# Turning differential attention's stacks and summing its head norms with float32r products

## The chip, the cores and the metric

One core of a Trainium2 chip runs the whole program in one launch. The metric is device time in microseconds (us) of that core. Three runs of the kernel before gave 1991.06, 1992.38 and 1996.98 us; their median is 1992.38 us.

Five engines matter here. TensorE (PE) multiplies: a stationary tile is loaded into the array (the profile calls this load PEld) and a moving tile is streamed past it. VectorE (DVE) and ScalarE (ACT) do element-wise work, and each engine works through its own instructions in their order in the program. SyncE (SP) issues the transfers.

## The reference

Two layers act on 256 latent tokens and 256 context tokens of width 1024, in float32. Each layer is a half-step SwiGLU, a mixer and a second half-step SwiGLU, each behind an RMS norm that is shifted and scaled. The mixer runs four groups of heads side by side on one input projection and joins them in one output projection. The change touches two of the groups. In short:

```
# differential attention: 8 score heads of 32 features make 4 output heads of 64
q, k = rope(rms(q)), rope(rms(k))
o    = softmax(q0 k0) v - lam * softmax(q1 k1) v      # for each pair of score heads
y    = rms(o) * subln * (1 - lam_init)                # a "head norm"
# HGRN2: a gated two-way scan of 4 heads of 64 value features
y    = rms(o) * out_norm * silu(g)                    # the other "head norm"
# both of them, with latent attention and grouped attention
x    = x + gate * concat(y...) @ mix_w_out
```

In the last layer the mixer gives only the latent half, 256 tokens instead of 512.

## The kernel before

**Dense products.** Activations and weights are kept as two float32r parts, hi and lo, and a dense product is three float32r products (`mm3`, or its like in `tokmajor`): hi by hi, hi by lo, lo by hi. Feature tiles are 128 rows by up to 512 tokens. `split` (line 246) makes the two parts: ACT copies a tile to float32r, and DVE subtracts that copy from the source.

**The mixer** (line 1026) is a long stream of dense products (`dense()`: the input projection, `mixin` in the trace, then the output projection, `mixo`) with chains of dependent steps woven into it. A chain is a generator that stops between its steps. Class `Weave` (line 101) writes the order: it keeps one clock for each of PE, DVE and ACT, adds a rough price for each instruction (`Engine.price`, line 70: 0.11 for a transpose, 0.00042 per column of a product, four times that where its moving operand is float32), adds a price per hop from one engine to another, and runs a chain's next step once its results should be there by those clocks. At most 4 chains (layer 0) or 3 (layer 1) are open at a time. A scheduler then places the instructions of every engine. So a changed instruction changes the clocks, and with them the order of everything woven in.

**The chains of this change.** In `da` (line 1148), `stack` writes for each tile of 128 tokens and each of two groups of four score heads a tile that holds q or k of a head as hi and lo parts, 4 times 32 columns; the parts are exact float32r numbers. `to_feat` (line 951) turns the k stacks and line 1187 the q stacks: a `transpose` on PE against the fp32 identity (`cst` in the trace), 128x128 each, four to a PSUM tile. In the trace these are `da0~pb<-cst,da0~g` and `da1~pb<-cst,da1~g`, one for each layer. `unit` (line 966) then makes the scores (`dau~ps`), the softmax, the transposes of the probabilities (`dau~pb<-cst,dau~g`) and the products with the values. When all units of a pair of output heads are done, `headnorm` (line 893) is spawned: ACT squares the pair's tile, PE multiplies the squares by a block matrix of ones (`self.blk`, also in `cst`) in one fp32 product, ACT makes `rstd` of the sums by a logarithm and an exponential, DVE scales. There are four head norms in a layer, `y0` and `y1` (differential attention, also called by its tile `da0~g` in the trace) and `y4` and `y5` (HGRN2, `hg0` and `hg1` in the trace).

**The output projection** takes its eight k tiles in two parts: 2, 3, 0, 1, 4, 6 and then 7, 5 (`MO` and `PARTS`). Tiles 2 and 3 come from latent attention, 6 and 7 from grouped attention (`gqa0`, `gqau`). Each part has eight output tiles. A first-part tile accumulates 18 products; four PSUM banks are open for them, so 4 times 15 products can run before tile 6 is there. In layer 0 a product has 512 columns, in layer 1 it has 256.

Of the kernel before, what the change touches and what calls it, by code (L numbers as in the profile page):

```python
# [15 lines left out]
P = 128  # L16
D = 1024
KT = 8
# [5 lines left out]
# per layer: chains at a time, their margin behind the products, lead of the other engines, price of a hop  # L24
# [22 lines left out]
# columns of the broadcast row of small weights  # L47
# [11 lines left out]
# of the output projection: the k tiles of each part, and the feature tiles that share a piece of its weights  # L59
# [4 lines left out]
class Engine:  # L64
    """An engine of the core; adds up a rough cost of what it is given, to order independent chains."""
# [35 lines left out]
class Weave:  # L101
    """Interleaves a long stream of dense products with chains of dependent steps."""
# [14 lines left out]
    def step(self, gen, ready):  # L117
        """Run one step; the time at which its results are there, None at its end."""
# [51 lines left out]
class Net:  # L170
    def __init__(self, tc, I, O, ctx):
# [29 lines left out]
        self.blk = self.cst[:, C_BLK:C_BLK + P]  # L201
        self.eps = self.cp.tile([P, 1], F32, tag="eps", name="eps")
# [43 lines left out]
    def split(self, hi, lo, src):  # L246
        """hi + lo == src, both exact in float32r."""
        nc = self.nc
        nc.scalar.activation(hi, src, AF.Copy)
        nc.vector.tensor_sub(lo, src, hi.bitcast(F32))  # L250

    def weights(self, src, fine=1):
        """A [P, <= 1024] piece of a weight as its two exact float32r parts."""
# [11 lines left out]
    def table(self, name):  # L265
        """Load an activation table behind all that ScalarE has been given."""
        self.tc.keep_in_program_order(self.bass.scalar.preload_act_table_set(name))

    def copy(self, out, src, scale=None):
        """out = src * scale (a value per partition), on the engine that is behind."""  # L270
# [18 lines left out]
    def rstd(self, out, ssum, n):  # L289
        """out = (ssum / n + eps) ** -0.5"""  # L290
        nc = self.nc
        p = ssum.shape[0]
        nc.scalar.activation(out, ssum, AF.Ln, bias=self.eps[:p], scale=1.0 / n)
        nc.scalar.activation(out, out, AF.Exp, scale=-0.5)

# [1 line left out]
    def ada_fin(self, l, m, mod, rv, f):  # L297
        """Bias, norm weight and step on the features f of the products rv [P, f, s]."""
# [5 lines left out]
        if m % 3 == 1:  # L304
            # norm_w * (1 + scale)
# [15 lines left out]
    def turned(self, row):  # L321
        """[P, f * P] sums, four rows of them in use -> [P, f, P], features on the partitions."""
# [6 lines left out]
    def ada_first(self, q):  # L329
        """A list of closures; run in order they give quarter q of the features of mods[0, 1] and mods[0, 0];  # L330
        products on the tensor engine, a column group to each module and parity of the k tile."""
# [29 lines left out]
    def ada_units(self, l, m):  # L361
        """A list of closures; run in order they give mods[l, m] = [P, KT, 2] (products on VectorE)."""
# [42 lines left out]
    def stat(self, dt, cc, late=0):  # L405
        """Adds the squares of the columns cc of feature tile dt to the sums of the next norm."""
# [17 lines left out]
    def norm_rs(self, s):  # L424
        """1 / rms of the tokens of stream s, on all partitions."""
# [8 lines left out]
    def norm_apply(self, xh, xl, l, i, s, rs, ks):  # L434
        """Feature tiles ks of rms(x) * norm_w * (1 + scale) + shift of stream s in two float32r parts."""
# [10 lines left out]
    def norm_begin(self, l, i, c0):  # L446
        """The next normed and modulated streams: the latents now, the context at norm_end."""
# [18 lines left out]
    def residual(self, ps, gate, dt, s, stat, late=0):  # L466
        """X += gate * ps on stream s."""
# [7 lines left out]
    def parts(self, c0, halves):  # L475
        """Column ranges to run one after the other and their streams."""
# [7 lines left out]
    def ffn(self, l, j, c0, filler, final=False):  # L484
# [12 lines left out]
        def fill(t):  # L497
            """Runs what is due of the filler after another t of the time it is spread over."""
# [11 lines left out]
        def up(fts, order, ws=None):  # L510
            """Hidden tiles fts side by side; order: the steps (k tile, columns). Yields after each step."""
            pss = [(self.psa(), self.psa()) if n < 2 else (self.psb(), self.pss()) for n in range(len(fts))]
            ws = ws or {}
            # a start marks the whole bank as unwritten: one is enough where the halves take turns
# [19 lines left out]
        def open_up():  # L534
            """The first tiles while the shift and scale of the second half of the features come in."""
# [87 lines left out]
    def mix_setup(self, l):  # L623
        """Small weights of layer l on every partition, rotary tables with the norm weights in them."""
# [8 lines left out]
        # T1, T2: [P, tt, qk, d]  # L633
# [15 lines left out]
        # lambda  # L649
# [12 lines left out]
        # subln * (1 - lam_init), hg_out_norm per partition (64-feature rows twice)  # L662
# [6 lines left out]
    def lb_setup(self):  # L669
        """Lower bounds of the last layer: softmax over the two layers, [P, dir, head]."""  # L670
# [22 lines left out]
    def feats(self, srcs, cs, halves=False):  # L693
        """Pairs of feature-major [128, N] tiles of the combined input projection, from columns cs on."""
# [23 lines left out]
    def tokmajor(self, src, ncol, c_ctx, then, banks=None):  # L718
        """Token-major columns, ctx tokens from column c_ctx on; src(i) the i-th pair of k tiles.
        then(tt, ps) gets each token tile."""  # L720
# [18 lines left out]
    def sigmoid(self, e, f, x):  # L739
        """f = 1 / (1 + exp(-x)) with the functions of one table, e = exp(-x) (both within 1e-19 of 0)."""  # L740
# [11 lines left out]
    def hgrn_gate(self, l, h, i, ps, c0):  # L752
        """q (i = 0) or the gates f and keys k of direction i - 1, [dk, tokens]."""
# [15 lines left out]
    def hgrn_head(self, l, h, q, F, K, o, last):  # L769
        """The scan of a head as attention whose decays are products of gates over halving blocks."""  # L770
# [15 lines left out]
        def blocks(ps, A, B):  # L786
            """The products of the keys A and queries B of each block of 32: ps[key, tile, query of the block]."""
# [10 lines left out]
        for li, b in enumerate(LEVELS):  # L798
# [11 lines left out]
            else:  # L810
                # the keys of 64 with the queries of the second and of the first part of them (b = 32), or of the
                # other 64: together the whole tiles, but for the blocks of 32 on the diagonal
# [11 lines left out]
            # to blocks of 2 b  # L824
# [25 lines left out]
        # now blocks of 128: between the two tiles of a stream  # L850
# [7 lines left out]
        # from the context to the latents  # L858
# [14 lines left out]
        # values  # L873
# [19 lines left out]
    def headnorm(self, key, o, w, c0, gates=None, n=0):  # L893
        """RMSNorm of each of a pair of 64-feature heads on the partitions."""
        nc = self.nc
        self.ph = key
        sq, rs = self.g([P, N]), self.g([P, N])
        nc.scalar.activation(sq[:, c0:], o[:, c0:], AF.Square)
        yield
        self.ph = key  # L900
        ps = self.psb()
        nc.tensor.matmul(ps[:, c0:], self.blk, sq[:, c0:], start=True, stop=True)
# [9 lines left out]
    def rot(self, out, zn, t1, t2, nh, d):  # L912
        """out = rotary(zn * w); out, zn: [P, nh, d]; tables [P, d]."""
# [10 lines left out]
    def heads_norm(self, src, nh, d):  # L924
        """src (PSUM) [P, nh * d] -> src / rms over d, [P, nh, d]."""
# [10 lines left out]
    def qk_tok(self, n, tt, ps, o, nq, nk, d, out):  # L936
        """Norm, weight and rotate the q and k heads of a token tile; out: [P, nq + nk, d]."""
# [12 lines left out]

    def to_feat(self, dst, toks, cols, np_, mask=None):
        """dst [np_, N] = transpose of toks[tt][:, cols]; toks[tt] may be None. With a mask, dst[i] keeps
        the rows that column i of it names."""
# [3 lines left out]
        for t in range(t0, 4):  # L957
            nc.tensor.transpose(ps[:np_, t], toks[t][:, cols], self.ident)
# [525 lines left out]
```

## Time and profile before

| what | value |
|---|---|
| runs | 1991.06, 1992.38, 1996.98 us, median 1992.38 us |
| span of the profiled execution, first to last instruction | 1989.2 us |
| PE busy | 1943.7 us, 98% |
| DVE busy | 1332.2 us, 67% |
| ACT busy | 908.3 us, 46% |
| mixer of layer 0, first product of `mixin0` to first of `ffn01` | 409.2 to 775.3 us |
| mixer of layer 1, first product of `mixin1` to first of `ffn11` | 1518.1 to 1795.4 us |

The page gives no time of the profiled execution beside its span; the three runs lie 1.9 to 7.8 us above that span. How to read it: busy times of PE hold the whole latency of a product, and the products overlap. What a product costs in a row of products is the distance from its start to the start of the next one, so the timeline is the view for it.

### The profile page before, as it was taken

Reading aid. Unit: us, or ns where it says so; the run is one execution under the profiler, and the core shown is the slowest. Engines: PE = TensorE matmul, PEld = TensorE weight load, DVE = VectorE, ACT = ScalarE, POOL = GpSimd, SP = SyncE. Lnnn points to the kernel's source line nnn. Section 1 sums busy time; section 2 is a strip of 40 time slices with the busy share of each in tenths; the row PEclk is TensorE's granted clock in tenths of the full one; section 3 lists DMA queues with packets and bytes.
Section 4 is the critical chain, followed back from the end, with each engine's and each line's share of the span. In section 5 each row is a group of like instructions: output and inputs, shape, how many; then the busy total and the mean of one; then the engine's idle time right before and its main releaser. Section 6 shows DMA issues by size and latency. Waiting matters only on the chain.

```text
span 1989.2 us, 30652 instructions
## 1 busy us (share of the span) xinstructions
PE 1943.7 (98%) x11929; PEld 1612.7 (81%) x11929; DVE 1332.2 (67%) x2706; ACT 908.3 (46%) x1826; POOL 0.2 (0%) x4
## 2 busy tenths in 40 slices
PE   6999999999999799999999999999999999899999
PEld 5888888897777578888888898888889877689999
DVE  5688678465768957875477467676656577876554
ACT  4332223355778775322223343222235577875443
POOL 0000000000000000000000000000000000000000
PEclk9999999999999999999999999999999999999999
DMA  8565556423011102654554335465543312125564
GB/s 281 173 200 179 175 172 185 124 80 119 23 62 33 45 28 80 193 162 141 159 181 147 118 107 178 150 191 156 157 121 120 109 49 70 44 85 161 167 196 123
DMA packets 87600, 260.82 MB, mean 131 GB/s; under 512 B 9248, under 2 KB 21280, under 8 KB 87456
## 3 DMA queue, kind: packets, MB, share of 16 engines
q1 hardware_dynamic: 87456, 258.88, 41.6%
q8 instruction: 93, 1.52, 0.3%
q14 instruction: 51, 0.42, 0.1%
HBM read 257.79 MB, written 1.05 MB: 130 GB/s over the span
## 4 chain that ended last, share of the span: by engine, by line
PE 92%; ACT 3%; DVE 2%; DMA 1%; issue 0%; SPq 0%; DVEq 0%; ACTq 0%
PE ffn01~pa L88 12%; PE ffn10~pa L88 12%; PE ffn00~pa L88 10%; PE mixin0~pa L88 7%; PE ffn11~pa L88 6%; PE mixin1~pa L88 5%; PE ffn00~ps L88 3%; PE ffn10~ps L88 3%; PE ffn01~ps L88 3%; PE ffn00~pb L88 3%; PE ffn10~pb L88 3%; PE ffn01~pb L88 3%; PE mixo0~pa L88 2%; PE ffn11~pb L88 2%; PE ffn11~ps L88 2%; PE hg0~ps L88 1%
## 5 line engine op out<-in xcount | busy, mean ns | idle before, releaser
L88 ACT ACTIVATE ffn10~whi<-ffn10~raw 128x1024 fp32r<-128x1024 f32 (+1 forms) x76 | 72.0, 950 | 165.6 <-PE ffn10~pa L88 46.7
L88 ACT ACTIVATE ffn01~whi<-ffn01~raw 128x1024 fp32r<-128x1024 f32 (+1 forms) x76 | 72.0, 950 | 165.4 <-PE ffn01~pa L88 50.6
L88 ACT ACTIVATE ffn00~whi<-ffn00~raw 128x1024 fp32r<-128x1024 f32 (+1 forms) x73 | 68.7, 945 | 171.2 <-DMA ffn00~raw<-win 69.9
L88 PE MATMUL ffn01~pa<-mixo0~xh,ffn01~whi 128*128 128x512 f32 (+1 forms) x384 | 142.7, 373 | 1.2 <-ACT mixo0~xh L88 1.2
L88 PE MATMUL ffn01~pa<-mixo0~xl,ffn01~whi 128*128 128x512 f32 (+1 forms) x384 | 142.8, 372 | 0.0
L88 PE MATMUL ffn10~pa<-ffn01~xh,ffn10~whi 128*128 128x512 f32 (+1 forms) x384 | 142.6, 373 | 0.0
L88 PE MATMUL ffn10~pa<-ffn01~xl,ffn10~whi 128*128 128x512 f32 (+1 forms) x384 | 142.5, 372 | 0.0
L88 PE MATMUL ffn01~pa<-mixo0~xh,ffn01~wlo 128*128 128x512 f32 (+1 forms) x384 | 142.5, 372 | 0.0
L88 PE MATMUL ffn10~pa<-ffn01~xh,ffn10~wlo 128*128 128x512 f32 (+1 forms) x384 | 142.3, 372 | 0.0
L88 DVE TENSOR_TENSOR ffn10~wlo<-ffn10~raw,ffn10~whi 128x1024 fp32r<-128x1024 f32 (+1 forms) x76 | 82.1, 1083 | 69.5 <-ACT ffn10~whi L88 69.1
L88 DVE TENSOR_TENSOR ffn01~wlo<-ffn01~raw,ffn01~whi 128x1024 fp32r<-128x1024 f32 (+1 forms) x76 | 82.1, 1083 | 64.7 <-ACT ffn01~whi L88 64.2
L88 DVE TENSOR_TENSOR ffn11~wlo<-ffn11~raw,ffn11~whi 128x1024 fp32r<-128x1024 f32 (+2 forms) x80 | 82.5, 1038 | 58.4 <-ACT ffn11~whi L88 58.4
L88 DVE TENSOR_TENSOR ffn00~wlo<-ffn00~raw,ffn00~whi 128x1024 fp32r<-128x1024 f32 (+1 forms) x73 | 78.5, 1077 | 62.4 <-ACT ffn00~whi L88 62.3
L88 PE MATMUL ffn00~pa<-init~xh,ffn00~whi 128*128 128x512 f32 x304 | 118.8, 391 | 0.0
L88 PE MATMUL ffn00~pa<-init~xh,ffn00~wlo 128*128 128x512 f32 x304 | 118.4, 389 | 0.0
L88 PE MATMUL ffn00~pa<-init~xl,ffn00~whi 128*128 128x512 f32 x304 | 118.3, 389 | 0.0
L88 DVE SCALAR_TENSOR_TENSOR ada~g<-ffn00~adaw,cs,ada~g 128x512 f32<-128x512 f32 x168 | 115.0, 749 | 0.0
L88 ACT ACTIVATE ffn11~whi<-ffn11~raw 128x1024 fp32r<-128x1024 f32 (+2 forms) x80 | 72.4, 910 | 64.1 <-issue 29.9
L88 PE MATMUL ffn11~pa<-mixo1~xh,ffn11~whi 128*128 128x256 f32 x352 | 99.2, 283 | 2.1 <-ACT mixo1~xh L88 2.1
L88 PE MATMUL ffn11~pa<-mixo1~xl,ffn11~whi 128*128 128x256 f32 x352 | 99.5, 283 | 0.0
L88 PE MATMUL ffn11~pa<-mixo1~xh,ffn11~wlo 128*128 128x256 f32 x352 | 99.3, 283 | 0.0
L88 DVE SCALAR_TENSOR_TENSOR ada~g<-ffn01~adaw,cs,ada~g 128x512 f32<-128x512 f32 x140 | 95.8, 748 | 0.8 <-DMA ffn01~adaw<-ada_w 0.8
(567 smaller groups left out, 5190.9 us busy)
## 6 DMA issues: line engine op xcount, KB each, us to landing
ffn00~adaw<-ada_w SPq DMA_DIRECT2D x48, 512.0 KB, 3.7
ffn01~raw<-win SPq DMA_DIRECT2D x44, 512.0 KB, 4.0
ffn10~raw<-win SPq DMA_DIRECT2D x44, 512.0 KB, 3.8
ffn11~raw<-win SPq DMA_DIRECT2D x44, 512.0 KB, 4.2
ffn00~raw<-win SPq DMA_DIRECT2D x41, 512.0 KB, 4.3
ffn01~adaw<-ada_w SPq DMA_DIRECT2D x40, 512.0 KB, 3.8
ffn10~adaw<-ada_w SPq DMA_DIRECT2D x40, 512.0 KB, 3.7
norm00~adaw<-ada_w SPq DMA_DIRECT2D x16, 512.0 KB, 6.1
```

The lines of the kernel that those rows point to most:

```text
L88: return f(*a, **k)
```

## The change

1. A tile `rounded` is made at the start: the identity and the block matrix of ones as float32r, by two casts on DVE.
2. `turn` takes the place of the transpose in `to_feat` and at line 1187. Where its input is float32r it is a plain product: the stack is stationary, the float32r identity moves, 128 columns. Else it is the transpose as before. The stacks now stay float32r, so all turns of differential attention's q and k are products: 64 in layer 0, 48 in layer 1.
3. `headnorm` splits the squares in hi and lo (`split`: one instruction on ACT, one on DVE) and sums them by two float32r products in place of one fp32 product. It takes two more tiles of the shared pool of 36.

```diff
+        self.rounded = self.cp.tile([P, 2, P], F32R, tag="rounded", name="rounded")
+        nc.vector.tensor_copy(self.rounded[:, 0], self.ident)
+        nc.vector.tensor_copy(self.rounded[:, 1], self.blk)
...
     def headnorm(self, key, o, w, c0, gates=None, n=0):
...
         sq, rs = self.g([P, N]), self.g([P, N])
+        hi, lo = self.g([P, N], F32R), self.g([P, N], F32R)
         nc.scalar.activation(sq[:, c0:], o[:, c0:], AF.Square)
+        self.split(hi[:, c0:], lo[:, c0:], sq[:, c0:])
         yield
         self.ph = key
         ps = self.psb()
-        nc.tensor.matmul(ps[:, c0:], self.blk, sq[:, c0:], start=True, stop=True)
+        nc.tensor.matmul(ps[:, c0:], self.rounded[:, 1], hi[:, c0:], start=True, stop=False)
+        nc.tensor.matmul(ps[:, c0:], self.rounded[:, 1], lo[:, c0:], start=False, stop=True)
         self.rstd(rs[:, c0:], ps[:, c0:], 64)
...
+    def turn(self, out, x):
+        if x.dtype == F32R:
+            self.nc.tensor.matmul(out, x, self.rounded[:, 0], start=True, stop=True)
+        else:
+            self.nc.tensor.transpose(out, x, self.ident)
...
-            nc.tensor.transpose(ps[:np_, t], toks[t][:, cols], self.ident)
+            self.turn(ps[:np_, t], toks[t][:, cols])
...
-                return st.rearrange("p h a d -> p h (a d)").bitcast(F32)
+                return st.rearrange("p h a d -> p h (a d)")
...
-                        nc.tensor.transpose(pt[:, h], sq[:, h], self.ident)
+                        self.turn(pt[:, h], sq[:, h])
```

The prices by which the order is written change with it: a turn of 128 columns has 0.054 in place of 0.11, and a head norm's product 2 x 0.215 in place of 0.86 at 512 columns. Three places show what this moves.

First, PE in layer 0 around `y0`'s sum, before. The `mixin0~pa` rows are dense products of the input projection, the `dau~ps` rows scores of differential attention.

```order
L88 MATMUL mixin0~pa_6406<-mixin0~wlo_6363,ffn00~xh_3339 128x512
L88 MATMUL mixin0~pa_6406<-mixin0~whi_6362,ffn00~xl_3340 128x512
L88 MATMUL dau~ps_6166<-da0~g_5784,da0~g_5946 128x256
L88 MATMUL dau~ps_6179<-da0~g_5777,da0~g_6002 128x512
L88 MATMUL dau~ps_6186<-da0~g_5784,da0~g_6002 128x512
L88 MATMUL y0~pb_6193<-y0~g_6173,cst 128x512
L88 MATMUL hg0~ps_6198<-hg0~g_6110,hg0~g_6111 32x32 x16
L88 MATMUL dau~pb_6294<-cst,dau~g_6121 128x128 x2
L88 MATMUL dau~ps_6267<-da0~g_5672,da0~g_6076 128x512
L88 MATMUL dau~ps_6274<-da0~g_5679,da0~g_6076 128x512
L88 MATMUL dau~pb_6299<-cst,dau~g_6164 128x128 x2
L88 MATMUL mixin0~pa_6555<-mixin0~whi_6260,ffn00~xh_3339 128x512
```

And now; the first row is the last product of the input projection.

```order
L88 MATMUL mixin0~pa_6622<-mixin0~whi_6242,ffn00~xl_3343 128x512
L88 MATMUL hg0~ps_6481<-hg0~g_6405,hg0~g_6406 32x32
L88 MATMUL dau~pb_6425<-cst,dau~g_6257 128x128 x2
L88 MATMUL dau~pb_6444<-cst,dau~g_6194 128x128 x4
L88 MATMUL dau~pb_6451<-cst,dau~g_6303 128x128 x4
L88 MATMUL hg0~ps_6481<-hg0~g_6405,hg0~g_6406 32x32 x12
L88 MATMUL dau~pb_6475<-dau~g_6423,vi_3403 64x128
L88 MATMUL dau~pb_6475<-dau~g_6428,vi_3403 64x128
```

After two more rows like the last two and three products of `hg0~ps` follow the two products of `y0`'s sum. Before, 48 products of the input projection stood behind `y0`'s sum; now none does. Likewise 24 products of the output projection now stand ahead of `y1`'s sum, where none stood.

Second, PE in layer 1 around `y5`'s sum, the last head norm, before. The `gqau~pb` rows with `gqa1~g` are grouped attention's last products with the values, the `mixo1~pa` rows the output projection's.

```order
L88 MATMUL gqau~pb_16740<-gqau~g_16713,gqa1~g_16039 64x128
L88 MATMUL gqau~pb_16740<-gqau~g_16720,gqa1~g_16039 64x128
L88 MATMUL y5~pb_16753<-y5~g_16750,cst 128x256
L88 MATMUL mixo1~pa_16856<-mixo1~g_16295,mixo1~wlo_16853 128x256
L88 MATMUL mixo1~pa_16856<-mixo1~g_16299,mixo1~whi_16852 128x256
L88 MATMUL mixo1~pa_16856<-mixo1~g_16300,mixo1~whi_16852 128x256
```

And now; `mixo1~g_16627` and `_16628` are the parts of tile 6, the first part's last.

```order
L88 MATMUL mixo1~pa_16925<-mixo1~g_16627,mixo1~whi_16921 128x256
L88 MATMUL y5~pb_16737<-y5~g_16726,rounded 128x256
L88 MATMUL gqau~pb_16771<-cst,gqau~g_16656 128x128 x4
L88 MATMUL mixo1~pa_16925<-mixo1~g_16628,mixo1~whi_16921 128x256
L88 MATMUL mixo1~pa_16925<-mixo1~g_16627,mixo1~wlo_16922 128x256
L88 MATMUL y5~pb_16737<-y5~g_16727,rounded 128x256
L88 MATMUL gqau~pb_16778<-cst,gqau~g_16687 128x128 x4
L88 MATMUL gqau~pb_16785<-gqau~g_16715,gqa1~g_16076 64x128
L88 MATMUL gqau~pb_16785<-gqau~g_16722,gqa1~g_16076 64x128
```

Before, 31 products of the first part stood behind `y5`'s sum; now the first part is done when its second product starts, and four transposes and 16 products with the values stand between that and the second part.

Third, DVE in layer 1 at the same place, before: the lo part of tile 7 (first row) stands ahead of `y5`'s scaling (second row), and the lo part of tile 5 is the last row.

```order
L88 TENSOR_TENSOR mixo1~g_16903<-gqa1~g_16411,mixo1~g_16902 128x256
L88 SCALAR_TENSOR_TENSOR mixin1~g_15479<-mixin1~g_15479,pvec,y5~g_16751 128x256
L88 SCALAR_TENSOR_TENSOR X<-mixo1~pa_16856,mod_5_11443,X 128x256
L88 TENSOR_TENSOR mixin1~g_15479<-mixin1~g_15479,mixin1~g_13844 128x256
L88 TENSOR_TENSOR ffn11~wlo_17051<-ffn11~raw_17048,ffn11~whi_17050 128x512 x2
L88 TENSOR_TENSOR mixo1~g_16907<-mixin1~g_15479,mixo1~g_16906 128x256
```

And now; the first row is the lo part of `y5`'s squares, which the change adds.

```order
L88 TENSOR_TENSOR y5~g_16727<-y5~g_16724,y5~g_16726 128x256
L88 SCALAR_TENSOR_TENSOR X<-mixo1~pa_16925,mod_5_11466,X 128x256
L88 TENSOR_TENSOR ffn11~wlo_17108<-ffn11~raw_17105,ffn11~whi_17107 128x512 x2
L88 SCALAR_TENSOR_TENSOR mixin1~g_15485<-mixin1~g_15485,pvec,y5~g_16725 128x256
L88 TENSOR_TENSOR mixin1~g_15485<-mixin1~g_15485,mixin1~g_13867 128x256
L88 TENSOR_TENSOR mixo1~g_16946<-gqa1~g_16473,mixo1~g_16945 128x256
L88 TENSOR_TENSOR mixo1~g_16950<-mixin1~g_15485,mixo1~g_16949 128x256
```

The lo part of tile 7 has moved behind `y5`'s scaling and gate.

## Rows read from the trace of the kernel before

**Rows 1.** The page: busy us of PE, its share, instructions; clock by slice.
```profile
PE 1943.7 (98%) x11929; PEld 1612.7 (81%) x11929; DVE 1332.2 (67%) x2706; ACT 908.3 (46%) x1826; POOL 0.2 (0%) x4
```
**Rows 2.** Windows: stretch, busy us of PE, PEld, DVE, ACT, POOL, granted clock, DMA.
```profile
620.00:640.00 20.00, 20.00 (x189) 15.93 (x188) 17.29 (x48) 17.05 (x43) 0.00 (x0) 1.00 0.14 41
640.00:660.00 20.00, 17.39 (x139) 11.43 (x136) 17.51 (x52) 18.24 (x51) 0.00 (x0) 1.00 0.00 1
660.00:680.00 20.00, 15.70 (x314) 12.00 (x313) 18.76 (x56) 16.50 (x43) 0.00 (x0) 0.97 0.22 66
680.00:700.00 20.00, 16.18 (x155) 12.11 (x154) 18.36 (x71) 10.65 (x29) 0.00 (x0) 0.86 0.16 47
...
1700.00:1720.00 20.00, 16.83 (x159) 11.77 (x158) 16.45 (x51) 17.61 (x46) 0.00 (x0) 0.91 0.01 2
1720.00:1740.00 20.00, 15.20 (x113) 10.88 (x112) 17.46 (x61) 15.26 (x48) 0.00 (x0) 0.92 0.29 86
```
**Rows 3.** Timeline of PE, layer 0: start us, us, what, shapes, count.
```profile
578.41 0.60 PE L88 MATMUL da0~pb<-cst,da0~g 128*128 128x128 f32 x4
578.85 0.39 PE L88 MATMUL hg0~ps<-hg0~g,mixin0~g 128*128 128x128 f32 x2
579.07 0.60 PE L88 MATMUL da0~pb<-cst,da0~g 128*128 128x128 f32 x4
579.42 0.48 PE L88 MATMUL mixin0~pa<-ffn00~xh,mixin0~whi 128*128 128x512 f32 x1
```
**Rows 4.** Timeline of PE, layer 1: float32r products of 256 and 512 columns.
```profile
1653.88 0.28 PE L88 MATMUL mixin1~pa<-ffn10~xh,mixin1~wlo 128*128 128x256 f32 x1
1654.00 0.40 PE L88 MATMUL mixin1~pa<-ffn10~xh,mixin1~whi 128*128 128x512 f32 x1
1654.23 0.40 PE L88 MATMUL mixin1~pa<-ffn10~xl,mixin1~whi 128*128 128x512 f32 x1
```
**Rows 5.** Groups of weight loads by form: count, busy us, mean ns.
```profile
L88 PEld LDWEIGHTS ffn10~pa<-ffn01~xl,ffn10~whi 128*128 128x128 f32 x384 | 72.4, 188 | 12.5 <-DVE ffn01~xl L88 0.2
...
L88 PEld LDWEIGHTS da0~pb<-cst,da0~g 128*128 128x128 f32 x64 | 7.5, 141 | 3.0 <-issue 1.5 <-ACT mla0~g L88 0.3 <-PE mixin0~pa L88 0.2
```
**Rows 6.** Chain that ended last, layer 0: start us, us, what.
```profile
602.89 0.86 PE y4~pb L88 x2
...
657.68 0.48 PE dau~ps L88 x2
...
667.15 0.25 PE mixin0~pa L88
...
680.66 1.71 PE y1~pb L88 x2
...
691.34 3.06 PE mixo0~pa L88 x10
```
**Rows 7.** The same chain, end of layer 1's mixer.
```profile
1720.26 0.43 PE y4~pb L88 x2
...
1780.19 0.63 PE y5~pb L88 x2
1780.83 7.14 PE mixo1~pa L88 x59
```
**Rows 8.** Groups of ACT and DVE by form: parts of a tile, 512 and 256 columns.
```profile
L88 ACT ACTIVATE mixo0~g<-da0~g 128x512 fp32r<-128x512 f32 x2 | 1.1, 622 | 0.0
...
L88 DVE TENSOR_TENSOR mixo0~g<-da0~g,mixo0~g 128x512 fp32r<-128x512 f32 x2 | 1.4, 700 | 0.0
...
L88 DVE TENSOR_TENSOR mixo1~g<-da1~g,mixo1~g 128x256 fp32r<-128x256 f32 x2 | 0.8, 420 | 0.0
```
**Rows 9.** Timeline of the start, DVE and PE.
```profile
6.04 3.61 DVE L88 TENSOR_TENSOR norm00~g<-norm00~g,norm00~g 128x256 f32<-128x256 f32 x7 [4.90 <-ACT norm00~g L88]
...
12.95 0.81 PE L88 MATMUL norm00~pb<-norm00~g,cst 128*128 128x256 f32 x2
```

## The prediction

> **What bounds the kernel now.** I read the busy times first, then the windows over both mixers, then the chain of waits there, and last the timeline and the groups by form for durations. PE is busy for 98% of the span [rows 1], so at first sight every nanosecond taken off PE is won. The windows show where that is not so: in nearly the whole mixer a stretch of 20 us has 20.00 us of PE, as the one at 620 us, but from 640 to 700 us and from 1700 to 1740 us PE has only 15 to 17 us, while DVE has 16.5 to 18.8 and ACT up to 18.2 [rows 2]. There, at the end of each input projection, the dense products have run out or stand in PE's queue behind a chain's product, and DVE and ACT set the pace. The granted clock falls too, to 0.86 in the worst of these stretches [rows 2]; since the clock has two levels, 1.2 and 2.4 GHz, this is a part of the stretch at the lower one, granted after PE had idled. So a saving on PE counts in full where PE is full, and work added to ACT and DVE counts in these five stretches.
>
> **The turns.** 64 and 48 transposes, 112 in all, become float32r products of 128 columns. Four transposes take 0.44 us from start to the next start (578.41 to 578.85) [rows 3], 0.110 us each. No row has a float32r product of 128 columns. What rows have: 512 columns take 0.23 us and 256 take 0.12 [rows 4], which by a straight line leaves 0.065 for 128; this is the lower end, if the streaming sets the time. An fp32 product of this very shape takes 0.22 (578.85 to 579.07, two records) [rows 3]; this is the upper end. Between them stands the weight load. Every turn has its own stationary tile, and a float32r load has a mean of 188 ns where the load of a transpose has 141 [rows 5]: it is 47 ns longer, about as long as the stream of 128 columns is shorter. I take 0.120, the spacing of the nearest row, 256 columns, on the reading that the load no longer hides behind so short a stream. The turns lie where PE is full in the stretch at 620 us [rows 2], so they count in full: 112 x (0.120 - 0.110) = +1.1 us. The ends are 112 x (0.065 - 0.110) = -5.0 and 112 x (0.22 - 0.110) = +12.3 us.
>
> The load rows can be set beside a rule of the Trainium skill, "TensorE: Matmul & The Clock Gate", section "LDWEIGHTS (loading the stationary operand)": a load takes its number of columns divided by 1.2, in ns, whatever the contraction; that is 107 for 128 columns. By it a turn could not fall below 0.107, and the 112 would give -0.3 us. The trace agrees in that the float32r load is the long one; its 188 ns hold a latency too.
>
> The same page, section "Back-to-back issue gap", has about 81 ns for one of a stream of load and product pairs at 128 columns. By it the turns would give 112 x (0.081 - 0.110) = -3.2 us, an estimate. The trace is above that page's gap where it can be seen, 0.23 us at 512 columns [rows 4] for the page's 216 ns.
>
> **The head norms' products.** An fp32 product of 512 columns takes 0.86 us and one of 256 takes 0.43 [rows 6, 7]; two float32r products take 2 x 0.23 and 2 x 0.12 [rows 4]. That is 0.40 less in layer 0 and 0.19 less in layer 1. Of the eight, I count those where PE has work behind it: y4 in layer 0 at 602.9 us and y5 in both layers, -0.40 - 0.40 - 0.19 = -1.0 us. The other five lie where PE waits anyhow [rows 2] and count nothing; if all eight counted it would be 4 x 0.40 + 4 x 0.19 = -2.4, if none 0.
>
> **The split of the squares.** It adds an ACT step of 622 ns and a DVE step of 700 ns to each norm of layer 0, and a DVE step of 420 ns to each of layer 1 [rows 8] with an ACT step that I estimate at 0.4 us from the ratio of the DVE rows. In a chain they stand between the squares and the sum, so y's sum comes that much later, and PE has them in order: what is queued behind the first sum product waits too. The least is 0: the order has moved the sums back, and the steps fit into gaps. The most is both steps of all eight on the path, 4 x 1.32 + 4 x 0.82 = 8.6 us. I take the DVE step alone, in the stretches where DVE is short: y0 and y1 in layer 0, y4, y0 and y1 in layer 1, 2 x 0.70 + 3 x 0.42 = +2.7 us. For y4 of layer 0 and both y5 the cover is PE's dense products; without it they cost up to 1.32 + 1.32 + 0.82 us, which the 8.6 holds.
>
> **The casts** stand on DVE among the sums of the first norm. Those end at 9.65 us and PE takes them up at 12.95 [rows 9], so two casts of 128 columns cost nothing; without this gap they would cost less than 0.7 us, what a step four times as wide takes [rows 8].
>
> **The order.** Nothing outside the mixers moves. In them the chains of differential attention now stand later among the dense products: 48 products of the input projection that stood behind y0's sum are now ahead of it, and y1's sum has 24 products of the output projection ahead of it. At the end of layer 1, y5's sum has lost its 31 products of cover. Both ways work is only exchanged: before y0 PE no longer idles for the chain, and behind it there is less to fill the next wait. PE's idle time in the five stretches is 2.6 + 4.3 + 3.8 + 3.2 + 4.8 = 18.7 us, and the clock's share there is (0.03 + 0.14 + 0.09 + 0.08) x 20 = 6.8 us [rows 2]. A change of order can move a third of the idle time either way, an estimate from no more than these rows: -6 to +6 us. I take 0.
>
> **The sum.** +1.1 - 1.0 + 2.7 + 0 = +2.8 us, on the profiled span of 1989.2 us 1992.0. The median of the runs lies 3.2 us above that span; the difference carries over, so 1992.4 + 2.8 = 1995.2 us. With the middle half of the order's term the forecast's own range is 1990 to 2001.
>
> **Rivals.**
>
> Slower: the dense products run out too early in layer 0. On the chain the last scores at 657.7 us lead to y1's sum at 680.7, and from the last product of the input projection on the chain (667.4) to the first of the output projection (691.3) 24 us pass [rows 6]. If the 48 products, 48 x 0.23 = 11.0 us, are gone before the last units of differential attention have their scores, those units' waits are bare; the 24 products ahead of y1 give back 5.5. That leaves 5.5 us, and about 2.8 more for the lower clock that follows idling, as in the stretch at 680 us (0.14 x 20) [rows 2]. For it: DVE is at 18 of 20 us there already and gets two splits more. Against it: the output projection starts on y0, which comes before y1. It decides once those 24 us grow. 1995.2 + 8.3 = 2003.5 us.
>
> Faster: a turn is bounded by its stream, 0.065 us, and the splits fit in gaps. For it: the loads of transposes hide today though they are 141 ns long and start every 110 ns [rows 3, 5]. Against it: the longer load. 1995.2 - 6.1 - 2.7 = 1986.4 us.
>
> Slower too: below 256 columns a float32r product is no faster than an fp32 one, 0.22 us. For it: no row shows that it is; against it: nothing between 512 and 256 columns bends. 1995.2 + 11.2 = 2006.4 us.
>
> **How the numbers follow.** 0.3%, about what a measurement of this kernel can tell from no change, is 6.0 us: faster ends at 1986.4 and slower begins at 1998.4. Forecast 0.50 (within 0.39, slower 0.09, faster 0.02); early end of the dense products 0.20 (slower 0.17, within 0.03); stream-bound turns 0.18 (faster 0.12, within 0.06); turns as slow as fp32 0.12 (slower 0.10, within 0.02). In sum faster 0.14, within 0.50, slower 0.36. The range takes in all three rivals' times, and at the lower end some order luck: 1985 to 2007.
>
> **What would show it.** In the timeline of the changed kernel the distance of `da0~pb` products: 0.12 us is my reading, 0.07 the faster rival's, 0.2 the slower's. Head norm sums two by two at 0.23 and 0.12 us. In the windows, PE's busy time behind the last product of the input projection, and the clock there; in the chain, the time from that product to the first of the output projection against 24 us. At the end of layer 1, whether PE idles between y5's sum and the next norm. I am wrong if the difference sits in the order alone, more than 6 us either way, with the turns near 0.12.

## The result: slower by 0.6%

The changed kernel takes 2005.1 us (median of 4 runs, 2004.69 to 2005.72) where the kernel before takes 1992.5 (4 runs). The ratio is 1.0059, 95% interval 1.0045 to 1.0072: some 12 us slower, twice the 0.3% that counts as no change here. The profiled execution has a span of 2002.6 us against 1989.2.

TensorE of the changed kernel has 6 us more busy time on the page than before, though the sums are shorter, and its share has fallen:

```profile
PE 1950.0 (97%) x11929; PEld 1620.9 (81%) x11929; DVE 1336.2 (67%) x2716; ACT 912.3 (46%) x1834; POOL 0.2 (0%) x4
```

Where the time went is read from one tile's first and last start (form: least/median/most ns of one, then first and last start). `ffn01` opens behind layer 0's mixer, `ffn11` behind layer 1's. Before:

```profile
L88 PE MATMUL ffn01~pa<-mixo0~xh,ffn01~whi x384: 274/389/499, 775.3 to 1083.6; 128*128 128x512 f32 x160, 128*128 128x256 f32 x32
...
L88 PE MATMUL ffn11~pa<-mixo1~xh,ffn11~whi x352: 278/283/387, 1795.4 to 1953.7; 128*128 128x256 f32 x176
```

After:

```profile
L88 PE MATMUL ffn01~pa<-mixo0~xh,ffn01~whi x384: 278/389/499, 778.6 to 1086.8; 128*128 128x512 f32 x160, 128*128 128x256 f32 x32
...
L88 PE MATMUL ffn11~pa<-mixo1~xh,ffn11~whi x352: 278/283/579, 1806.4 to 1967.0; 128*128 128x256 f32 x176
```

By layer 0's end 3.3 us are lost (0.7 of them ahead of its mixer, whose first product starts at 409.9 instead of 409.2), by layer 1's 11.0, and 2.3 more in `ffn11`, whose first products run at up to 579 ns instead of 387. So layer 1 lost more than twice what layer 0 did. The windows answer to [rows 2] (stretch, busy us of PE, PEld, DVE, ACT, POOL, granted clock). Three stretches of layer 1 before, which [rows 2] does not have:

```profile
1660.00:1680.00 20.00, 20.00 (x155) 15.59 (x147) 16.17 (x48) 17.12 (x39) 0.00 (x0) 1.00 0.13 40
...
1740.00:1760.00 20.00, 19.15 (x198) 14.86 (x198) 15.08 (x50) 13.57 (x39) 0.00 (x0) 0.99 0.00 1
...
1800.00:1820.00 20.00, 20.00 (x169) 20.00 (x169) 12.08 (x17) 12.19 (x19) 0.00 (x0) 1.00 0.52 162
```

After:

```profile
640.00:660.00 20.00, 19.52 (x188) 14.54 (x186) 17.63 (x60) 18.55 (x54) 0.00 (x0) 1.00 0.01 2
660.00:680.00 20.00, 11.73 (x190) 8.01 (x190) 19.31 (x49) 15.14 (x41) 0.00 (x0) 0.89 0.35 109
680.00:700.00 20.00, 17.81 (x190) 13.74 (x183) 18.39 (x82) 14.59 (x41) 0.00 (x0) 0.77 0.01 2
...
1660.00:1680.00 20.00, 19.21 (x153) 15.54 (x152) 15.53 (x45) 17.06 (x45) 0.00 (x0) 0.89 0.18 46
...
1740.00:1760.00 20.00, 17.30 (x156) 13.94 (x156) 15.65 (x57) 12.40 (x43) 0.00 (x0) 0.83 0.13 42
...
1800.00:1820.00 20.00, 16.50 (x106) 15.57 (x106) 12.11 (x24) 10.24 (x20) 0.00 (x0) 0.83 0.29 89
```

Read two columns together. In layer 0 the idle time has mostly moved: 640 to 660 us has filled up, 660 to 680 has emptied to 11.7 of 20 us. But the granted clock is lower in more places than before. At the lower level, 1.2 GHz, a product of 512 columns starts every 0.42 us instead of every 0.23 (rows in the third part of the experiments), so a busy us does about half the work there, and PE can be busy for longer with less to do.

The turns come near my reading of 0.120 us. Timeline of PE after (start, us):

```profile
586.21 0.63 PE L88 MATMUL da0~pb<-rounded,da0~g 128*128 128x128 f32 x4
586.68 0.44 PE L88 MATMUL mixin0~pa<-ffn00~xh,mixin0~whi 128*128 128x512 f32 x1
```

Four turns take 0.47 us, the hand-over to the next product included; the median from one to the next is 0.113 us, where a transpose had 0.109. The sums are two by two at 0.23 and 0.12 us where nothing holds them up: on the chain `y1` has both in 0.46 us.

### The profile page after: what moved, and what is told of

Same layout as the page of the kernel before. It is cut to its first block, busy times and chain, and to the rows that moved or that the text cites. A ratio compares the mean times of both kernels' runs of the same rounds, so it can differ in the third digit from the quotient of the medians.

```text
span 2002.6 us, 30675 instructions
## 1 busy us (share of the span) xinstructions
PE 1950.0 (97%) x11929; PEld 1620.9 (81%) x11929; DVE 1336.2 (67%) x2716; ACT 912.3 (46%) x1834; POOL 0.2 (0%) x4
## 4 chain that ended last, share of the span: by engine, by line
PE 92%; ACT 3%; DVE 3%; issue 1%; DMA 1%; SPq 0%; DVEq 0%
PE ffn01~pa L88 12%; PE ffn10~pa L88 12%; PE ffn00~pa L88 10%; PE mixin0~pa L88 7%; PE ffn11~pa L88 6%; PE mixin1~pa L88 5%; PE ffn00~ps L88 3%; PE ffn10~ps L88 3%; PE ffn01~ps L88 3%; PE ffn00~pb L88 3%; PE ffn10~pb L88 3%; PE ffn01~pb L88 3%; PE mixo0~pa L88 2%; PE ffn11~pb L88 2%; PE ffn11~ps L88 2%; PE hg0~ps L88 1%
```

## The experiments

Thirteen kernels stand against the kernel before. Two numbers go with most of what they lose: TensorE's idle time in the two mixers and their ends (490 to 800 and 1620 to 1830 us; length minus busy time, from the windows), and the clock's loss there (length times one minus the granted clock, to two digits; an upper bound, since a low clock under an idle engine costs nothing). Both are from one profiled execution for each kernel, whose span is in the last column, and that need not be a typical one: p6, p8 and e3 were profiled in the longest of their 5, 12 and 6 executions, e8 in the shortest of 10, and before near its shortest. So the two numbers are to be set beside the span, and not beside the ratio.

| kernel | ratio to before, 95% | as us | idle us | clock us | its span, us |
|---|---|---|---|---|---|
| before | 1 | | 25.9 | 7.3 | 1989.2 |
| **changed** | 1.0059 (1.0045 to 1.0072) | +11.8 | 31.9 | 18.8 | 2002.6 |
| e1 turns alone, new prices | 1.0050 (1.0037 to 1.0064) | +10.0 | 28.9 | 12.5 | 2002.2 |
| e2 head norms alone | 1.0031 (1.0021 to 1.0042) | +6.2 | 30.5 | 14.6 | 1997.6 |
| e3 full, old prices | 1.0046 (1.0032 to 1.0059) | +9.2 | 27.7 | 20.9 | 2006.0 |
| e4 old instructions, new prices | 1.0001 (0.9992 to 1.0011) | +0.2 | 25.1 | 13.5 | 1992.4 |
| p3 full, old order | 1.0051 (1.0038 to 1.0065) | +10.2 | 29.7 | 15.6 | 2002.0 |
| p4 old instructions, new order | 1.0054 (1.0041 to 1.0067) | +10.8 | 30.9 | 14.6 | 2000.8 |
| p5 turns, old order | 0.9996 (0.9987 to 1.0005) | -0.8 | 25.9 | 7.3 | 1989.8 |
| p6 head norms, old order | 1.0061 (1.0049 to 1.0074) | +12.2 | 30.8 | 15.6 | 2004.9 |
| p7 split that nobody waits for | 1.0012 (1.0004 to 1.0021) | +2.4 | 26.9 | 10.4 | 1994.2 |
| p8 turns, one rounded sum | 0.9997 (0.9989 to 1.0005) | -0.6 | 26.8 | 12.5 | 1995.4 |
| e5 turns alone, old price | **0.9979 (0.9969 to 0.9988)** | -4.2 | 21.0 | 7.3 | 1986.7 |
| e8 turn's price mended, sums later | 1.0029 (1.0020 to 1.0039) | +5.8 | 28.4 | 15.6 | 1996.2 |

The mean granted clock is on record for every execution. Its median is 0.994 for before, 0.995 and 0.996 for p5 and e5, 0.993 and 0.992 for p7 and p8, and 0.988 to 0.991 for all that lose 5.8 us or more. But e4 has 0.989 and loses nothing: a low clock goes with the losses, and is not the price by itself.

The windows behind three of the rows. Before:

```profile
490.00:800.00 310.00, 296.81 (x2585) 229.58 (x2584) 232.00 (x652) 227.93 (x563) 0.00 (x0) 0.99 0.15 48
1620.00:1830.00 210.00, 197.29 (x1633) 160.96 (x1632) 157.30 (x420) 154.13 (x375) 0.00 (x0) 0.98 0.26 81
```

Changed:

```profile
490.00:800.00 310.00, 295.23 (x2561) 229.45 (x2560) 234.44 (x657) 231.04 (x566) 0.00 (x0) 0.98 0.15 46
1620.00:1830.00 210.00, 192.84 (x1558) 155.64 (x1552) 153.89 (x427) 151.98 (x381) 0.00 (x0) 0.94 0.22 69
```

e5:

```profile
490.00:800.00 310.00, 300.51 (x2597) 231.48 (x2596) 234.32 (x656) 229.76 (x567) 0.00 (x0) 0.99 0.15 49
1620.00:1830.00 210.00, 198.49 (x1640) 163.30 (x1639) 156.25 (x409) 152.86 (x369) 0.00 (x0) 0.98 0.26 83
```

### First: parts and prices

Theory 1: the new order costs it. Theory 2: the instructions do.

e1 keeps the turns and takes the head norms back, to the changed kernel:

```
-        hi, lo = self.g([P, N], F32R), self.g([P, N], F32R)
-        self.split(hi[:, c0:], lo[:, c0:], sq[:, c0:])
...
-        nc.tensor.matmul(ps[:, c0:], self.rounded[:, 1], hi[:, c0:], start=True, stop=False)
-        nc.tensor.matmul(ps[:, c0:], self.rounded[:, 1], lo[:, c0:], start=False, stop=True)
+        nc.tensor.matmul(ps[:, c0:], self.blk, sq[:, c0:], start=True, stop=True)
```

e2 is the reverse; a stack is an fp32 tile again, so it is turned by a transpose:

```
-                return st.rearrange("p h a d -> p h (a d)")
+                return st.rearrange("p h a d -> p h (a d)").bitcast(F32)
```

> The turns of the stacks are float32r products; the head norms are as before, one fp32 product of unsplit squares. Theory 1 (the order): what costs the 12.6 us is the order in which the weave lays chains and dense products, since the planner now charges a turn 0.054 us where it charged 0.11. Counted over the instruction list of TensorE, 1397 rows of this kernel stand elsewhere than before (1583 with the whole change), so theory 1 expects most of the loss here: 2000 to 2006 us, ratio 1.004 to 1.007, with more stretches at half clock than the 13.6 us of before in the mixers. Theory 2 (the instructions: the split of the squares on ScalarE and VectorE with the waits behind it): this kernel has no split and its turns are 0.004 us each longer, 112 of them, so 1993 us, ratio 1.000 to 1.001.

> The head norms split their squares and sum them in two float32r products; the turns stay fp32 transposes. Theory 1 (the order): 648 rows of TensorE's list stand elsewhere than before, less than half as many as with the turns alone, so 1992 to 1998 us, ratio 1.000 to 1.003. Theory 2 (the instructions): all of the split is here, so 2002 to 2006 us, ratio 1.005 to 1.007, with the time gone in front of the sums y0, y1, y4 and y5.

e1 took 2005.0 us, e2 2000.9. Theory 1 has e1 right, theory 2 would have had 1993; e2 lies between both.

e3 has the whole change at the old prices: the planner's clocks are set back behind each new step (here a turn and the split; the two sums likewise).

```
+            pe = self.nc.cost["pe"]
             self.nc.tensor.matmul(out, x, self.rounded[:, 0], start=True, stop=True)
+            self.nc.cost["pe"] = pe + 0.11
...
+        c = dict(nc.cost)
         self.split(hi[:, c0:], lo[:, c0:], sq[:, c0:])
+        nc.cost.update(c)
```

e4 has none of the change, and its prices (at a stack's transpose, and in the head norm):

```
+                        nc.cost["pe"] += 0.00042 * P - 0.11
...
+        nc.cost["act"] += 0.07 + (N - c0) / 1200.0
+        nc.cost["dve"] += 0.06 + (N - c0) / 960.0
+        nc.cost["hops"] += 1
...
+        nc.cost["pe"] -= 0.00042 * 2 * (N - c0)
```

> All instructions of the change, but the planner is charged what it was charged before: 0.11 us a turn, the fp32 price for the two float32r sums, nothing for the split. TensorE's list differs from that of before in 504 rows, from that of the changed kernel in 1522. Theory 1 (the order): 1991 to 1997 us, ratio 0.999 to 1.002. Theory 2 (the instructions): 2002 to 2006 us, ratio 1.005 to 1.007.

> All instructions of before, but the planner is charged as in the changed kernel: 0.054 us a turn, half the price for a head norm's sum, and the split's prices on ScalarE and VectorE that are not issued. TensorE's list differs from that of the changed kernel in 512 rows, from that of before in 1460. Theory 1 (the order): 2001 to 2006 us, ratio 1.004 to 1.007. Theory 2 (the instructions): 1990 to 1995 us, ratio 0.999 to 1.001.

e3 took 2004.3 us and e4 1995.5: both about as theory 2 has it, against e1. The contradiction has a cause in the kernels: prices do not fix the order. The scheduler behind the weave lays the instructions anew when they change. So e3, with the old prices, still has some 380 rows of TensorE's list elsewhere than before (504 by the wider count of its expectation), and e4 differs from the changed kernel in 512 by that wider count.

### Second: the order held

So I held the order itself. Each engine's instructions got an order-only edge to the one ahead of it in the wanted list, for PE, DVE and ACT; only added instructions are free. The weave's prices are those of the kernel whose order is wanted.

```
+        for a, b in zip(place, place[1:]):
+            tc.add_manual_dep(given[b], given[a].name, mybir.DependencyInfo(
+                mybir.DependencyClass.NoSync, mybir.DependencyReason.DATA), reason="pin")
```

Apart from the added instructions no row of the lists stands elsewhere than in the kernel whose order is held.

> Only the turns are float32r products, the head norms are as before, and all three engines are held to the order of the kernel before. Theory 1 (the order): 1993 to 1997 us, ratio 0.999 to 1.001. Theory 2 (the instructions): the run with the turns alone lost 10 us, so 2000 to 2006 us, ratio 1.003 to 1.006. By the spacing of the turns, 0.113 us for 0.109, 112 of them, the price would be 0.5 us.

> Only the head norms are changed (split squares, two float32r sums), the turns stay transposes, and all three engines are held to the order of the kernel before but for the added instructions. Theory 1 (the order): 1993 to 1997 us, ratio 0.999 to 1.001. Theory 2 (the instructions): the run with the head norms alone lost 6 us, so 1998 to 2002 us, ratio 1.002 to 1.004, with the time gone behind the split, in front of the sums of y0, y1, y4 and y5.

> All instructions of the change, and TensorE, VectorE and ScalarE are each held to the order of the kernel before, instruction by instruction; only the added ones (8 second products, 8 splits on each of ScalarE and VectorE, 2 casts) find their own place. The run with the old prices still had 383 rows of TensorE's list elsewhere than before, so its loss of 9 us could still be order. Theory 1 (the order, whichever planner makes it): 1993 to 1997 us, ratio 0.999 to 1.001. Theory 2 (the instructions themselves): 2001 to 2006 us, ratio 1.003 to 1.006.

> All instructions of the kernel before, and all three engines are held to the order of the changed kernel, which lacks here only the added instructions. Theory 1 (the order): 2003 to 2008 us, ratio 1.004 to 1.007. Theory 2 (the instructions): 1993 to 1998 us, ratio 0.999 to 1.002.

1991.8, 2005.0, 2003.7 and 2003.2 us. Neither theory has all four, and p6 (2005.0) lies above both. The turns cost nothing that can be seen by themselves, and neither does holding the order, as p5 comes out like before; the changed kernel held to its own order was not run. The head norms alone cost the whole loss in the old order. And the old instructions alone cost nearly the whole loss in the new order. Either is enough, and together they cost no more than one: 11.8 us, not 10.8 + 12.2.

p4's waits are those of the changed kernel. PE's longest waits in 1620 to 1830 us (tile, what it waited for, us, times, longest), changed kernel:

```profile
PE hg1~ps L88 <- DVE hg1~attc L88: 2.7, 2, 2.4
...
PE y1~pb L88 <- ACT y1~g L88: 1.8, 1, 1.8
PE norm12~pb L88 <- ACT mixo1~g L88: 1.4, 1, 1.4
PE gqau~pb L88 <- ACT y5~g L88: 1.3, 1, 1.3
```

p4, without one instruction of the change:

```profile
PE hg1~ps L88 <- DVE hg1~attc L88: 2.8, 2, 2.4
...
PE gqau~pb L88 <- ACT y5~g L88: 1.5, 1, 1.5
PE norm12~pb L88 <- ACT mixo1~g L88: 1.4, 1, 1.4
...
PE y1~pb L88 <- ACT y1~g L88: 0.9, 1, 0.9
```

The same list. Only at `y1` does the changed kernel, with the split, wait 0.9 us longer. Before has little at the first and at `norm12`, and nothing at the other two:

```profile
PE hg1~ps L88 <- DVE hg1~attc L88: 0.4, 1, 0.4
...
PE norm12~pb L88 <- DVE mixo1~g L88: 0.2, 1, 0.2
```

p6 has other waits, at the sums and at the scores near them. Those of its list that grew most, 490 to 800 us, then 1620 to 1830:

```profile
PE dau~ps L88 <- ACT dau~g L88: 2.0, 3, 1.2
...
PE y0~pb L88 <- ACT y0~g L88: 0.7, 1, 0.7
PE y1~pb L88 <- ACT y1~g L88: 0.6, 1, 0.6
...
PE y0~pb L88 <- ACT y0~g L88: 2.6, 1, 2.6
...
PE y1~pb L88 <- DVE y1~g L88: 1.1, 1, 1.1
```

Before, two of them occur:

```profile
PE dau~ps L88 <- ACT dau~g L88: 0.8, 2, 0.6
...
PE y0~pb L88 <- ACT y0~g L88: 1.3, 1, 1.3
```

That is 4.9 us of new waits, and by 4.9 us idle time grew; smaller waits, some longer and some shorter, about cancel. The span of this execution is 15.7 us above that of before. Of these 2.8 lie ahead of the mixers, whose first product starts at 412.0 us instead of 409.2, and the rest goes with the clock, whose loss is up to 15.6 us for 7.3. In the median p6 loses 12.2.

### Third: which part of the head norm, and the price of a turn

p7 issues the split but sums the unsplit squares in fp32, so nothing waits for it. p8 writes the squares as float32r at once, leaves their lo parts out and sums them in one product. Both hold the old order.

p7's sum, to p6's:

```
-        nc.tensor.matmul(ps[:, c0:], self.rounded[:, 1], hi[:, c0:], start=True, stop=False)
...
+        nc.tensor.matmul(ps[:, c0:], self.blk, sq[:, c0:], start=True, stop=True)
```

p8's, to p3's:

```
-        sq, rs = self.g([P, N]), self.g([P, N])
+        sq, rs = self.g([P, N], F32R), self.g([P, N])
...
+        nc.tensor.matmul(ps[:, c0:], self.rounded[:, 1], sq[:, c0:], start=True, stop=True)
```

> As the run with the head norms alone in the order of before (which lost 10.9 us), but nothing waits for the split: ScalarE and VectorE still do its 8 copies and 8 differences, and the sum is the fp32 product of the unsplit squares. TensorE's order is exactly that of before. Theory 2a (the wait: in the old order the sum stands as soon as the squares are there, and with the split it waits for a copy, a difference and two hand-overs, about 1 us each time, and the clock falls behind it): 1992 to 1997 us, ratio 0.999 to 1.0015. Theory 2b (the added work on ScalarE and VectorE holds up what else is queued there, as the copy behind which a product of layer 0 waited 1.2 us): 2000 to 2005 us, ratio 1.003 to 1.006.

> The turns as changed, and the head norms' squares written as float32r and summed in one product: no split, no low parts (they are left out of the sum). Order of all three engines as before. If the split is all that costs, 1988 to 1995 us, ratio 0.997 to 1.0005: the eight sums are shorter by 0.63 us (512 columns, 0.86 to 0.23) and 0.31 us (256 columns, 0.43 to 0.12), 3.8 us together if all of it is on the path. Were the float32r products themselves the cause (by whatever they do to the clock), 2000 to 2005 us.

p7 took 1996.6 us, p8 1992.7. The 16 added steps on ACT and DVE cost 2.4 us; the other 10 us of p6 come with the two float32r sums that wait for them (theory 2a; the two sums without the wait were not run). And p8, whose sums are 3.8 us shorter in all, gains nothing that can be seen over p5 (+0.2 us, give or take some 2.4). The place of `y0`'s sum in layer 0 shows what can take the saving back. Timeline of PE in the kernel before ([idle before it, and what ended it]):

```profile
647.62 1.13 PE L88 MATMUL y0~pb<-y0~g,cst 128*128 128x512 f32 x2
...
652.25 0.50 PE L88 MATMUL mixin0~pa<-mixin0~whi,ffn00~xh 128*128 128x512 f32 x1 [1.78 <-ACT mixin0~g L88]
652.59 0.40 PE L88 MATMUL mixin0~pa<-mixin0~wlo,ffn00~xh 128*128 128x512 f32 x1
652.82 0.39 PE L88 MATMUL mixin0~pa<-mixin0~whi,ffn00~xl 128*128 128x512 f32 x1
```

p8:

```profile
649.50 0.50 PE L88 MATMUL y0~pb<-y0~g,rounded 128*128 128x512 f32 x1
650.17 0.46 PE L88 MATMUL hg0~ps<-hg0~g,hg0~g 128*32 128x32 f32 x32 [0.17 <-ACT dau~g L88]
...
651.33 0.73 PE L88 MATMUL dau~ps<-da0~g,da0~g 128*128 128x512 f32 x2 [0.34 <-ACT dau~g L88]
...
654.13 0.79 PE L88 MATMUL mixin0~pa<-mixin0~whi,ffn00~xh 128*128 128x512 f32 x1 [1.78 <-ACT mixin0~g L88]
654.73 0.63 PE L88 MATMUL mixin0~pa<-mixin0~wlo,ffn00~xh 128*128 128x512 f32 x1
655.15 0.63 PE L88 MATMUL mixin0~pa<-mixin0~whi,ffn00~xl 128*128 128x512 f32 x1
```

Behind the shorter sum PE waits for ACT, 0.17 and then 0.34 us, where it waited for nothing before. The products that follow start 0.42 or 0.43 us apart instead of 0.23. Windows 650 to 662 us, before, then p8, then p6:

```profile
650.00:662.00 12.00, 10.22 (x112) 7.47 (x112) 10.74 (x29) 11.76 (x30) 0.00 (x0) 1.00 0.01 1
```
```profile
650.00:662.00 12.00, 9.71 (x91) 7.07 (x91) 8.75 (x25) 10.73 (x28) 0.00 (x0) 0.72 0.00 0
```
```profile
650.00:662.00 12.00, 9.15 (x57) 6.11 (x57) 10.19 (x27) 11.12 (x27) 0.00 (x0) 0.72 0.00 0
```

With the fp32 sum the clock is 1.00 here (before, p5, p7), with float32r sums 0.72 (p3, p6, p8): three profiles to three, all in one order of TensorE. In p8 what PE does just ahead of it differs by the shorter sum and the waits behind it. But this does not show that the shorter sum lowers the clock. The same three profiles had a longer stretch of low clock near the start (last section), and their first mixer starts later (411.2, 412.0 and 411.5 us, against 409.2, 409.5 and 410.0). With one profile for each kernel, the sum and the course of that one execution cannot be told apart. What bears the sum out is that the mean clock of p8's executions is 0.990 to 0.993 in 11 of 12, and of p5's 0.994 to 0.996 in 10 of 11.

e5 is e1 with the old price of 0.11 us a turn and nothing held:

```
+            pe = self.nc.cost["pe"]
             self.nc.tensor.matmul(out, x, self.rounded[:, 0], start=True, stop=True)
+            self.nc.cost["pe"] = pe + 0.11
```

> Turns as float32r products charged at the old 0.11 us, head norms as before, nothing held: 578 rows of TensorE's list stand elsewhere than before, all by the scheduler that lays the instructions at build time, since the weave's prices are the old ones. The same instructions in the order of before cost nothing (ratio 0.9996), in the free order with the new prices 1.005. If the build-time scheduler's answer to the new instructions is what moves things for the worse: 2000 to 2005 us, ratio 1.003 to 1.006. If it takes the weave's new prices: 1991 to 1997 us, ratio 0.999 to 1.0015.

1989.2 us: 4.2 us below before, clear of its interval though under the 0.3%, and 14 us (0.7%) below e1, which neither expectation held. e1 and e5 differ in one price. The charge of 0.11 is what a turn takes (0.113); the change's 0.054 is its columns alone. That the better price makes the better order is shown for this pair only: e4 has the price of 0.054 and loses nothing, e3, with the split, has 0.11 and loses 9.2 us.

e8 is the changed kernel with that price, and one more step between the split and the sum:

```
         self.split(hi[:, c0:], lo[:, c0:], sq[:, c0:])
         yield
         self.ph = key
+        yield
+        self.ph = key
```

> The changed kernel with two corrections to what its planner is told, no instruction added or taken: a turn is charged 0.11 us (it takes 0.113) where the change charged 0.054, and the sum of a head norm is a planner's step (1 us) further behind its split, so that in layer 0 the sums of y4 and y0 stand some 30 rows later on TensorE than with the price alone. Theory 2a (the sum waits for its split, and the turn's price is wrong): 1991 to 1997 us, ratio 0.999 to 1.0015. If the loss is in any order that holds the split: as the head norms alone in free order, 1998 to 2003 us, ratio 1.002 to 1.004.

2001.0 us, as the head norms alone (e2): the miss is theory 2a's. With both corrections half the loss comes back, and no more than by leaving the turns out. The two were not run one by one. In no order that was run is a kernel whose sums wait for the split as fast as before.

## Why the prediction was right and wrong

**The time** of 2005.1 us is inside the range, but the forecast of 1995.2, no change, was not what happened. The range reached so far up for the rival of turns as slow as fp32 products (2006.4), which the runs rule out: that it holds the result is luck. Half of my sign of being wrong came true: the order by itself moves 10.8 us, more than my 6, with the turns at 0.113. The other half did not, as the head norms cost as much without it. By the forecast's steps:

- **The turns, +1.1.** Right within the noise: 0.113 us each where I took 0.120, and -0.8 us (-2.6 to +1.0) in the old order. Both rivals on them, 0.065 and 0.22 us, are out. The Trainium skill's "TensorE: Matmul & The Clock Gate", section "LDWEIGHTS (loading the stationary operand)", would have a turn at no less than 0.107 us; the trace agrees. The 0.081 us of its "Back-to-back issue gap" does not occur as the usual spacing here. The 216 ns that I set beside 0.23 us is that section's figure for a product by itself; for a stream of load and product pairs of 512 columns it has 131 ns, and the dense products here stand at 0.23 us.
- **The head norms' products, -1.0.** Nothing can be seen of it: p8 is 0.2 us above p5, give or take 2.4, with 3.8 us less in its sums. So 1.0 is not ruled out, but 3.8 is. I had counted the places where PE has work behind the sum; at `y0` part of the time saved became waiting all the same.
- **The split, +2.7, at most 8.6.** In the old order it is 12.2 us with the shorter sums, above my end. The waits, some 5 us, are within the bound. What failed is the step "the most is both steps of all eight on the path": it held no clock, and in p6's profile the clock's loss in the mixers is up to 8.3 us larger than before.
- **The order, "I take 0", -6 to +6.** This is the step that failed in the changed kernel: +10.8 us (p4). I took a third of the old idle time for what an order can move; idle time in p4's profile grew by 5.0 us, inside that, and the clock's loss by up to 7 on top, for which the step had no term. I had also seen the new order at `y5` and called it an exchange; `gqau~pb` waits 1.3 us there until ACT has read `y5`'s sum.
- **The sum.** I added terms of which the runs show that they do not add. Why the split costs so little in the new order (changed kernel against p4, 0.05%, with intervals of 0.13% either way) was not tried; that the planners laid this order around it is my reading.

**The slower rival**, the dense products running out in layer 0, has its mark: from the last start of an input product to the first of the output projection 28.9 us pass (661.3 to 690.2), before 21.0 (670.3 to 691.3). But the stretch begins 9 us earlier, and layer 0 lost 3.3 us, not 8.3. The rival's time of 2003.5 is near the result for another reason: layer 1, which I had not priced.

Open: which of the displaced rows in the new order cost the 10.8 us. And with one profile per kernel the split of a loss between idling and clock is rough, and why the clock fell where it did stays open.

## What to carry to other kernels

Where a planner orders the work, an instruction's price is part of the change, and it can be worth more than the instruction (14 us between e1 and e5). Before pricing a change by its instructions, hold the order and vary them, then hold them and vary the order; two causes that each explain a loss need not add. Shortening an instruction just ahead of a wait can come back as waiting (`y0` in p8). And see how far apart the executions of one kernel lie before reading one profile against another.

## What was not expected of the hardware

A float32r product of 128 columns with its own stationary tile starts every 0.113 us although its load shows 189 ns (141 for a transpose): of the 48 ns by which the load is longer, 4 show in the spacing. And the low stretch of the clock near the start is of three sizes in the same code: up to 50 us, before, e4, p7 and the changed kernel run the same steps in the same order on TensorE, VectorE and ScalarE, but for two casts in the last two. The mean clock there is 0.91 in 5 of the 14 profiles, 0.83 in 2 and 0.74 in 7. Windows 15 to 35 us, before, then p7, then e4:

```profile
15.00:35.00 20.00, 14.92 (x103) 11.18 (x102) 11.18 (x34) 8.88 (x19) 0.00 (x0) 0.91 0.94 307
```
```profile
15.00:35.00 20.00, 15.33 (x107) 11.36 (x100) 10.97 (x31) 8.96 (x20) 0.00 (x0) 0.83 0.92 299
```
```profile
15.00:35.00 20.00, 15.33 (x94) 10.60 (x87) 10.48 (x26) 8.80 (x20) 0.00 (x0) 0.74 0.85 275
```

The dense products of e4 are 2.7 us later from there on (the mixer's first at 411.9 us instead of 409.2); single profiles are not to be compared closer than that.
